# Hybrid decoder layer: memory's 1/rms moved behind its projections, and half of the gMLP value norm moved to ScalarE

## The chip, the cores and the metric

The kernel runs on one core of a Trainium2 chip. A core has five engines with a queue each: TensorE (PE; its weight loads are shown apart as PEld), VectorE (DVE), ScalarE (ACT), GpSimd (POOL) and SyncE (SP, which issues the DMAs here). Each works through its own queue in order and waits for others by semaphores. The metric is the device time of one execution in microseconds.

## What is computed

One layer of a decoder trunk for 1024 tokens of width 1024, in float32, with three sub-layers: a mixer (an S5 state-space group beside a gMLP spatial gate), cross-attention into 256 memory tokens, and a gated FFN with a causal convolution. The change touches two normalisations: that of the gMLP values, per head of 64, and that of the memory.

```python
def rmsnorm(x, g):
    xf = x.astype(jnp.float32)
    xf = xf * lax.rsqrt(jnp.mean(xf * xf, axis=-1, keepdims=True) + RMS_EPS)
    return xf.astype(x.dtype) * g

def chunked_spatial_gate(u, v, g_v, w_s, b_s):
    vh = v.reshape(bsz, nc, CHUNK, GMLP_HEADS, GMLP_HEAD_DIM)
    vh = rmsnorm(vh, g_v.reshape(GMLP_HEADS, GMLP_HEAD_DIM))
    mixed = jnp.einsum('hts,bnshd->bnthd', w_s * mask, vh) + b_s.T[None, None, :, :, None]
    return u * mixed.reshape(bsz, L, D_GMLP)

def memory_cross_attention(h, mem_n, w_q, w_k, w_v, w_o):
    k = (mem_n @ w_k).reshape(bsz, -1, XATTN_HEADS, XATTN_HEAD_DIM)
    v = (mem_n @ w_v).reshape(bsz, -1, XATTN_HEADS, XATTN_HEAD_DIM)
    ...

h = rmsnorm(x, g_mix_pre[l])
s_in, s_gate, g_u, g_vv = jnp.split(h @ w_in[l], splits, axis=-1)
...
mem_n = rmsnorm(mem, g_mem[l])
xa = memory_cross_attention(h, mem_n, w_q[l], w_k[l], w_v[l], w_o[l])
```

## The kernel before

**Products.** Activations lie transposed, channels on partitions and tokens along the row, in tiles of 128x512 (two halves of 512 tokens). Every float32 operand is split into a high part, rounded to the matmul's input type, and a low part that holds the rest; a product is three matmuls (high by high, high by low, low by high), made by `mm3` (L234). ACT makes the high part of a weight tile (the cast of L132), DVE or POOL subtracts it for the low part (L135); for activations the same pair is L253 and L254. Weight tiles come by DMA into four buffers `raw`, and their split parts lie in 13 buffers `w`, so a split waits until PE has done with an older tile.

**The stretch around the change.** In the mixer PE works through, in this order: projections of the S5 input and gate, the gMLP values (`vt`, eight tiles of 128 tokens by 512 channels, with the sums of squares per head in `vss`), gates 0 and 1 of gMLP (`gates`, evicted by the multiply of L1006), the mixing of values along the chunk (`mixing`, L1013, evicted by L1018), gates 2 and 3 (evicted by L1002), then the projections of memory to keys (eight blocks of 128 channels, evicted by ACT copies, L1051) and values (eight tiles, L1059). `v_norm` (L692 to L702) makes 1/rms per head on DVE and multiplies the eight tiles with it, one DVE instruction for a tile (L701), before the mixing.

Memory lies transposed in four tiles of 128x2x256 (two groups of 128 channels, 256 tokens). `mem_norm` makes 1/rms per token, first with tokens on partitions (`r`, one column for each 128 tokens), then spread over all partitions by small matmuls (`mem_bc`, 128x256). `mem_parts` loads a tile, multiplies each half by the gain (a value per partition) and `mem_bc` on DVE (L686), and splits it into high (ACT) and low (POOL).

**S5 beside it.** A side job runs along: eight batches of the state space (`s5_batch`, L540 to L623), each with transposes (L560, copied out by ACT at L564), a product (L575, copied out at L577), halves swapped by DMA, rotations on DVE and POOL (L588 to L597), the scans (L600), a second swap by DMA (L603, L604), the back rotation (L606 on DVE, L607 on POOL, L608 on DVE) and a last product (L618, L619), which reads what L608 wrote. The batches' outputs are read back at L652 and gated at L659.

**The order.** The program's text fixes which side job advances at which tick; then a scheduler in the compiler lays the instructions into the queues by its own estimate of their times. A small edit can thus move other instructions. From the end of the memory projections on the work of PE is the attention, the FFN and the down-projection; its order there is the same in both kernels.

Of the kernel before, what the change touches and what calls it, by code (L numbers as in the profile page):

```python
# [18 lines left out]
AF = mybir.ActivationFunctionType  # L19
ALU = mybir.AluOpType  # L20
AX = mybir.AxisListType

P = 128
# [129 lines left out]
class Builder:  # L153
# [517 lines left out]
    def mem_norm(self):  # L671

        r = yield from self.token_rms("mem", 2, "x")
        yield
        yield
        self.mem_bc = self.bcast(r, 2, "ac")[1]

    def mem_parts(self):
        nc, v, g = self.nc, self.nc.vector, self.nc.gpsimd
        bc = self.mem_bc  # L680
        self.memp = []
        for i in range(4):
            m = self.mem_load(i)
            for j in range(2):
                kt = 2 * i + j
                v.scalar_tensor_tensor(m[:, j], m[:, j], self.gain["g_mem"][:, kt:kt + 1], bc[:, :256],  # L686
                                       ALU.mult, ALU.mult)
            hl = self.pair("m", [P, 2, 256])
            self.split(*hl, m, g)
            self.memp.append(hl)  # L690
            yield

    def v_norm(self, vt, vss):

        nc, v, g = self.nc, self.nc.vector, self.nc.gpsimd
        v.tensor_scalar(vss, vss, 1.0 / 64, EPS, ALU.mult, ALU.add)
        r = self.rsqrt(vss, [P, 64])
        yield
        for i in range(8):
            v3 = vt[i].rearrange("p (h d) -> p h d", d=64)  # L700
            v.tensor_tensor(v3, v3, r[:, 8 * i:8 * i + 8].unsqueeze(2).to_broadcast([P, 8, 64]), ALU.mult)  # L701
            yield  # L702


# [192 lines left out]
    def mixers(self):  # L897
        nc, a, w, ids, xg = self.nc, self.a, self.w, self.ids, self.xg
        v, g = nc.vector, nc.gpsimd
# [4 lines left out]
        for kt in range(KT):  # L904
# [9 lines left out]
            for h in range(2):  # L914
                rh, rl = xg[h][kt]
                for b in range(2):
# [3 lines left out]
                    c = slice(256 * (kt % 2) + P * b, 256 * (kt % 2) + P * b + P)  # L920
# [13 lines left out]
        r = self.value(stat)  # L934
        rstd = [r[:, 4 * h:4 * h + 4] for h in range(2)]
        bc = [self.bcast(rstd[h], 4)[1] for h in range(2)]
# [12 lines left out]
        for b in range(2):  # L949
            part = self.blocks(ids["s"][b])  # L950
            for h in range(2):
                ps = self.bank("sx" if b == 0 else "acc")
# [6 lines left out]
        for b in range(4):  # L959
            part = self.blocks(ids["sg"][b])  # L960
            for h in range(2):
                ps = self.bank()
# [8 lines left out]
        for q in range(2):  # L971
            part = self.blocks(ids["gv"][q], 256)
            for i in range(8):
                ps = self.bank()[:, :256]
                h, c = i // 4, slice((i % 4) * P, (i % 4) * P + P)
# [69 lines left out]
        for b in range(8):  # L1045
            part = self.blocks(ids["k"][b])
            ps = self.bank()[:, :256]
            self.mm3(ps, [(*part(k), *memv(k)) for k in range(8)], ticks=1)
            if b % 2 == 0:
                self.kraw.append(self.slot("m", shape=[P, 2, 256]))  # L1050
            nc.scalar.copy(self.kraw[-1][:, b % 2], ps)  # L1051
        for c in range(4):
            part = self.blocks(ids["v"][c], 256)
            for mt in range(2):
                ps = self.bank()[:, :256]
                self.mm3(ps, [(*memv(k, slice(P * mt, P * mt + P)), *part(k)) for k in range(8)], ticks=1)
                if c % 2 == 0:
                    self.vraw[mt, c // 2] = self.slot("m")
                nc.scalar.copy(self.vraw[mt, c // 2][:, 256 * (c % 2):256 * (c % 2) + 256], ps)  # L1059
        self.memp = None  # L1060
        self.drain(s5)

# [593 lines left out]
```

## Time and the profile before

| | |
|---|---|
| runs | 1346.27, 1342.07, 1339.8 us, median 1342.07 |
| the profiled execution | 1340.39 us, its span 1338.7 us |
| PE, PEld | 1270.3 us (95%), 1076.9 us (80%) |
| DVE | 1062.5 us (79%) |
| ACT | 628.3 us (47%) |
| POOL | 691.0 us (52%) |
| mean granted PE clock | 0.977 |
| DMA | 233.56 MB, mean 174 GB/s |

The profile records one execution. Its span runs from the first to the last instruction; times in rows are counted from its start. A row of the timeline gives start, length, engine, line, operation, out<-in and count, and in brackets the idle time before it and what ended it. Instructions of one engine overlap a little, so the distance between two starts can be shorter than the length of one. A busy PE is not a PE at its peak, since the granted clock is part of it.

### The profile page before, as it was taken

How to read it: one execution, taken by the hardware profiler on the slowest of the kernel's cores; microseconds unless marked ns; L12 is line 12 of the kernel's file. 1: busy time of each engine (PE TensorE's matmuls, PEld its weight loads, DVE VectorE, ACT ScalarE, POOL GpSimd, SP SyncE). 2: the span in 40 equal slices, each digit the busy share in tenths (PEclk: the TensorE clock that was granted, in tenths of full speed). 3: DMA queues.
4: the chain of work that ended last, by engine and by line, in shares of the span. 5: the costliest groups of instructions: out<-in, count | busy, mean ns of one | idle time of the engine just before them, and what ended most of it. 6: DMA issues, size and time to landing. Idle time of an engine off the chain costs nothing. (4 is left out here: it accounts for less than half of the span.)

```text
span 1338.7 us, 19253 instructions
## 1 busy us (share of the span) xinstructions
PE 1270.3 (95%) x6356; PEld 1076.9 (80%) x6356; DVE 1062.5 (79%) x1627; ACT 628.3 (47%) x1176; POOL 691.0 (52%) x523
## 2 busy tenths in 40 slices
PE   9989998779999999889999999999999999999995
PEld 7778987678888788678888878888888888788885
DVE  7968989987558766996657988889998878995477
ACT  7233421245455444454545645555555555546341
POOL 1685445747644734630443838755565315763135
PEclk9989999879999999899999999999999999999997
DMA  9474435348826973451358566645555359666234
GB/s 319 139 206 113 114 95 166 86 125 306 288 94 200 319 244 89 125 187 56 91 163 296 162 222 233 186 144 161 154 167 164 103 162 379 190 201 210 72 92 157
DMA packets 150661, 233.56 MB, mean 174 GB/s; under 512 B 33697, under 2 KB 43041, under 8 KB 150561
## 3 DMA queue, kind: packets, MB, share of 16 engines
q1 hardware_dynamic: 150560, 232.34, 54.5%
q8 instruction: 49, 0.80, 0.3%
q14 instruction: 52, 0.42, 0.1%
HBM read 174.23 MB, written 53.85 MB: 170 GB/s over the span
## 5 line engine op out<-in xcount | busy, mean ns | idle before, releaser
L234 PE MATMUL acc<-b,w 128*128 128x512 f32 x2484 | 597.5, 393 | 10.0 <-DVE sq L965 3.4
L234 PEld LDWEIGHTS acc<-b,w 128*128 128x128 f32 x2484 | 466.6, 190 | 109.1 <-DVE sq L965 3.8
L135 DVE TENSOR_TENSOR w<-raw,w 128x512 fp32r<-128x512 f32 x206 | 203.9, 1000 | 92.6 <-PE acc L234 43.1
L234 PE MATMUL sx<-b,w 128*128 128x512 f32 x873 | 210.1, 390 | 0.7 <-ACT T L1303 0.6
L132 ACT CAST w<-raw 128x512 fp32r<-128x512 f32 x228 | 140.9, 621 | 132.7 <-PE acc L234 70.7
L234 PEld LDWEIGHTS sx<-b,w 128*128 128x128 f32 x873 | 163.6, 188 | 35.5 <-ACT T L1303 1.0
L234 PE MATMUL acc<-T,w 128*128 128x512 f32 x528 | 127.0, 389 | 0.0
L713 POOL TENSOR_TENSOR ac<-ac,sq 128x512 f32<-128x512 f32 x45 | 69.1, 1537 | 103.9 <-ACT sq L712 58.0
L234 PEld LDWEIGHTS acc<-T,w 128*128 128x128 f32 x528 | 99.1, 188 | 20.6
L254 DVE TENSOR_TENSOR w<-b,w 128x512 fp32r<-128x512 f32 x64 | 65.2, 1027 | 30.1 <-PE st L234 15.5
L731 POOL TENSOR_TENSOR m<-m,t 128x512 f32<-128x512 f32 x24 | 40.0, 1698 | 63.7 <-DVE m L730 50.7
L234 PE MATMUL sx<-T,w 128*128 128x512 f32 x264 | 66.5, 389 | 0.0
L234 PEld LDWEIGHTS sx<-T,w 128*128 128x128 f32 x264 | 49.6, 188 | 10.3
L712 ACT ACTIVATE sq<-m 128x512 f32<-128x512 f32 x66 | 41.0, 630 | 34.7 <-DVE ac L713 14.4
L116 POOL TENSOR_TENSOR st<-st,b 128x512 f32<-128x512 f32 x20 | 26.8, 1339 | 56.0 <-DMA st<-in_w_up 35.6
L1242 POOL TENSOR_TENSOR b<-b,m 128x512 f32<-128x512 f32 x22 | 32.2, 1466 | 44.9 <-ACT m L1241 44.7
L253 ACT CAST w<-b 128x512 fp32r<-128x512 f32 x64 | 39.6, 620 | 29.5 <-PE acc L234 18.1
L135 POOL TENSOR_TENSOR w<-raw,w 128x512 fp32r<-128x512 f32 x22 | 30.2, 1377 | 42.5 <-ACT w L132 24.7
L234 PE MATMUL acc<-w,b 128*128 128x256 f32 x384 | 49.3, 285 | 0.0
L1380 POOL TENSOR_TENSOR m<-m,m 128x512 f32<-128x512 f32 x28 | 39.3, 1410 | 18.9 <-DMA m<-in_w_dk 8.4
L730 DVE SCALAR_TENSOR_TENSOR m<-m,gains,st 128x512 f32<-128x512 f32 x32 | 44.5, 1457 | 3.3 <-ACT st L311 3.2
L234 PEld LDWEIGHTS acc<-w,b 128*128 128x128 f32 x384 | 47.0, 191 | 0.1
(360 smaller groups left out, 2335.5 us busy)
## 6 DMA issues: line engine op xcount, KB each, us to landing
raw<-in_w_up SPq DMA_DIRECT2D x68, 256.0 KB, 2.9
cd<-fd SPq DMA_DIRECT2D x44, 256.0 KB, 2.9
b<-sd SPq DMA_DIRECT2D x44, 256.0 KB, 3.9
b<-in_w_up SPq DMA_DIRECT2D x40, 256.0 KB, 2.8
raw<-in_w_out SPq DMA_DIRECT2D x32, 256.0 KB, 2.9
raw<-in_w_q SPq DMA_DIRECT2D x32, 256.0 KB, 2.8
raw<-in_w_o SPq DMA_DIRECT2D x32, 256.0 KB, 2.8
m<-in_w_dk SPq DMA_DIRECT2D x28, 256.0 KB, 4.7
```

What stands on the lines that cost most here:

```text
L116: g.tensor_tensor(p["S4"], p["12"], p["S2"], ALU.subtract)
L132: nc.scalar.copy(hi[:, :w], t[:, :w])
L135: e.tensor_tensor(lo[:, :w], t[:, :w], hi[:, :w], ALU.subtract)
L234: self.pin(nc.tensor.matmul(ps, lhsT=x, rhs=y, start=first and i + j == 0, stop=last and i == n - 1 and j == 2, skip_group_check=go_on))
L253: self.nc.scalar.copy(hi, src)
L254: (e or self.nc.vector).tensor_tensor(lo, src, hi, ALU.subtract)
L712: nc.scalar.activation(sq, src, AF.Square)
L713: (e or nc.gpsimd).tensor_tensor(acc, acc, sq, ALU.add)
L730: v.scalar_tensor_tensor(x, x, self.gain[gpost][:, i:i + 1], bc, ALU.mult, ALU.mult)
L731: g.tensor_tensor(x, x, rs, ALU.add)
L1242: nc.gpsimd.tensor_tensor(val, val, gate, ALU.mult)
L1380: g.tensor_tensor(t[to], t[x], t[y], op)
```

## The change

The values of gMLP: tiles 0, 2, 4, 6 are multiplied by DVE as before, tiles 1, 3, 5, 7 by ACT, head by head, each head with its own scale (eight ACTIVATEs of 128x64 per tile). The memory: the tiles get only the gain, on ACT, and 1/rms is applied where keys and values leave PSUM. For keys tokens lie along the row, so the eight ACT copies become DVE multiplies with `mem_bc`; for values tokens lie on partitions, so the ACT copies become ACTIVATEs with `mem_r` as scale.

```diff
         yield
         yield
+        self.mem_r = r
         self.mem_bc = self.bcast(r, 2, "ac")[1]
 
     def mem_parts(self):
         nc, v, g = self.nc, self.nc.vector, self.nc.gpsimd
-        bc = self.mem_bc
...
                 kt = 2 * i + j
-                v.scalar_tensor_tensor(m[:, j], m[:, j], self.gain["g_mem"][:, kt:kt + 1], bc[:, :256],
-                                       ALU.mult, ALU.mult)
+                nc.scalar.activation(m[:, j], m[:, j], AF.Identity, scale=self.gain["g_mem"][:, kt:kt + 1])
...
             v3 = vt[i].rearrange("p (h d) -> p h d", d=64)
-            v.tensor_tensor(v3, v3, r[:, 8 * i:8 * i + 8].unsqueeze(2).to_broadcast([P, 8, 64]), ALU.mult)
+            if i % 2:
+                for hd in range(8):
+                    nc.scalar.activation(v3[:, hd], v3[:, hd], AF.Identity, scale=r[:, 8 * i + hd:8 * i + hd + 1])
+            else:
+                v.tensor_tensor(v3, v3, r[:, 8 * i:8 * i + 8].unsqueeze(2).to_broadcast([P, 8, 64]), ALU.mult)
...
-            nc.scalar.copy(self.kraw[-1][:, b % 2], ps)
+            v.tensor_tensor(self.kraw[-1][:, b % 2], ps, self.mem_bc[:, :256], ALU.mult)
...
-                nc.scalar.copy(self.vraw[mt, c // 2][:, 256 * (c % 2):256 * (c % 2) + 256], ps)
+                nc.scalar.activation(self.vraw[mt, c // 2][:, 256 * (c % 2):256 * (c % 2) + 256], ps, AF.Identity,
+                                     scale=self.mem_r[:, mt:mt + 1])
```

From here on the file's lines are shifted: L701 of before is L704 (DVE) and L702 (ACT), L1002, L1006, L1013 and L1018 are L1005, L1009, L1016 and L1021, the eviction of keys L1051 is L1054, that of values L1059 is L1062. Lines up to L675 keep their numbers.

**Where the order moves.** First ACT's queue at the norm of v, before:

```order
L132 CAST w_2543<-raw_2298 128x512
L132 CAST w_2594<-raw_2333 128x512
L621 ACTIVATE x_1681<-sx 128x512
L564 COPY x_1713<-sx 128x512
L132 CAST w_2613<-raw_2368 128x512
L577 COPY x_1735<-sx 128x512
```

and after (m_1970 to m_1976 are tiles 1, 3, 5 and 7 of the values, `rs_y` their 1/rms; w_2601 is the weight tile that was w_2594, and w_2627 the one that was w_2613):

```order
L132 CAST w_2543<-raw_2298 128x512
L702 ACTIVATE m_1970<-m_1970,rs_y_2519 128x64 x8
L702 ACTIVATE m_1972<-m_1972,rs_y_2519 128x64 x8
L132 CAST w_2601<-raw_2333 128x512
L702 ACTIVATE m_1974<-m_1974,rs_y_2519 128x64 x8
L702 ACTIVATE m_1976<-m_1976,rs_y_2519 128x64 x8
L621 ACTIVATE x_1681<-sx 128x512
L564 COPY x_1713<-sx 128x512
L132 CAST w_2627<-raw_2368 128x512
L132 CAST w_2785<-raw_2516 128x512
L577 COPY x_1735<-sx 128x512
```

The thirty-two new instructions stand on both sides of one weight cast and ahead of L621 and L564, the copies out of PSUM of two S5 batches. On PE the reader of that copy, L575, moves back past the last seven matmuls of gate 1 and the first two of the mixing.

Next DVE's queue around the third L608 of this stretch (x_1780 is the S5 batch that it finishes), before:

```order
L600 SCALAR_TENSOR_TENSOR x_1780<-r_712,x_1735 128x128 x4
L659 TENSOR_TENSOR k_3135<-k_3125,k_3135 128x4x64
L135 TENSOR_TENSOR w_2758<-raw_2516,w_2757 128x512
L659 TENSOR_TENSOR k_3143<-k_3125,k_3143 128x4x64
L686 SCALAR_TENSOR_TENSOR sq_2813<-sq_2813,gains,ac_1042 128x256 x2
L606 TENSOR_TENSOR x_1780<-x_1780,x_1774 128x512
L135 TENSOR_TENSOR w_2784<-raw_2547,w_2783 128x512
L608 TENSOR_TENSOR x_1780<-x_1780,x_1737 128x512
```

and after:

```order
L600 SCALAR_TENSOR_TENSOR x_1780<-r_712,x_1735 128x128 x4
L1005 TENSOR_TENSOR sq_2825<-acc,st_753 128x512
L135 TENSOR_TENSOR w_2786<-raw_2516,w_2785 128x512
L606 TENSOR_TENSOR x_1780<-x_1780,x_1774 128x512
L608 TENSOR_TENSOR x_1780<-x_1780,x_1737 128x512
L135 TENSOR_TENSOR w_2812<-raw_2547,w_2811 128x512
L1005 TENSOR_TENSOR sq_2869<-acc,st_760 128x512
L659 TENSOR_TENSOR k_3163<-k_3153,k_3163 128x4x64
L659 TENSOR_TENSOR k_3171<-k_3153,k_3171 128x4x64
```

Besides the L686 that are gone, two L659 and one weight split have moved behind L608, and an eviction of a gate (L1002, now L1005) from ahead of the scans to behind them. The reader of L608 on PE, L619, moves ahead by eight matmuls of the gates.

Last, DVE's queue ahead of the fourth L608 (x_1860), before:

```order
L606 TENSOR_TENSOR x_1860<-x_1860,x_1854 128x512
L135 TENSOR_TENSOR w_3235<-raw_3082,w_3234 128x512
L254 TENSOR_TENSOR b_3031<-k_3026,b_3030 128x512
L254 TENSOR_TENSOR b_3049<-k_3044,b_3048 128x512
L608 TENSOR_TENSOR x_1860<-x_1860,x_1839 128x512
```

and after:

```order
L606 TENSOR_TENSOR x_1860<-x_1860,x_1854 128x512
L1054 TENSOR_TENSOR m_3120<-acc,ac_1042 128x256
L254 TENSOR_TENSOR b_3117<-k_3112,b_3116 128x512
L254 TENSOR_TENSOR b_3168<-k_3163,b_3167 128x512
L135 TENSOR_TENSOR w_3309<-raw_3209,w_3308 128x512
L254 TENSOR_TENSOR b_3176<-k_3171,b_3175 128x512
L1054 TENSOR_TENSOR m_3229<-acc,ac_1042 128x256
L608 TENSOR_TENSOR x_1860<-x_1860,x_1839 128x512
```

Five of the eight new evictions, three more weight splits than before and three more L254 now stand ahead of this L608 and behind the third. On PE its reader, L619, moves back by 44 matmuls of the key projection.

## The prediction, made blind

> **What bounds the kernel now.** TensorE (PE) is busy 95% of the span, so the first view is the list of waits, for PE, over the whole span. Columns: who waited for whom, total us, times, longest.
>
> ```profile
> PE sx L619 <- DVE x L608: 17.1, 5, 9.9
> PE acc L234 <- DVE w L135: 7.2, 7, 2.6
> PE acc L1013 <- DVE m L1006: 3.3, 1, 3.3
> ```
>
> All three name VectorE (DVE). Next the stretches, for where: us, then busy time and instructions of PE, PEld, DVE, ACT, POOL, granted PE clock, DMA share, GB/s.
>
> ```profile
> 250.00:275.00 25.00, 18.23 (x111) 16.99 (x111) 22.59 (x18) 9.16 (x17) 23.14 (x15) 0.81 0.25 74
> ...
> 300.00:350.00 50.00, 47.07 (x306) 42.57 (x305) 33.15 (x27) 24.39 (x48) 39.66 (x27) 1.00 0.91 317
> ```
>
> At 250 to 275 us PE idles 6.8 of 25 us, its clock is at 0.81, and DVE and POOL are nearly full; behind 300 us PE is the bound again. The timeline of PE gives the gaps (start, us, in brackets the idle time before, and who ended it):
>
> ```profile
> 206.47 1.05 PE L575 MATMUL sx<-x,x 128*128 128x128 f32 x8
> ...
> 215.63 1.97 PE L1013 MATMUL acc<-k,m 128*64 128x128 f32 x14 [3.26 <-DVE m L1006]
> ...
> 232.98 11.82 PE L234 MATMUL acc<-b,w 128*128 128x512 f32 x51
> 254.69 0.80 PE L619 MATMUL sx<-x,x 128*128 128x127 f32 x2 [9.89 <-DVE x L608]
> ...
> 290.79 0.80 PE L619 MATMUL sx<-x,x 128*128 128x127 f32 x2 [3.83 <-DVE x L608]
> ...
> 293.86 8.97 PE L234 MATMUL acc<-m,w 128*128 128x256 f32 x61
> ...
> 302.66 13.84 PE L234 MATMUL acc<-w,m 128*128 128x256 f32 x114
> ```
>
> These three gaps are 17.0 us (a fourth, for L135, is among the 7.2 above), between the gMLP gates and the end of the key projection at 302.66. Each also lowers the clock afterwards, as a short stretch behind the 9.89 us gap shows:
>
> ```profile
> 256.00:258.00 2.00, 2.00 (x11) 2.00 (x11) 2.00 (x3) 0.52 (x1) 2.00 (x2) 0.50 0.04 10
> ```
>
> So DVE's queue from 198 to 291 us sets the time here, and each of its microseconds ahead of an L608 counts. Behind 302.66 the PE order is unchanged and PE itself is nearly full, so what is won there I carry to the end.
>
> **The norm of v.** Eight DVE multiplies become four on DVE and thirty-two on ScalarE (ACT).
>
> ```profile
> 197.99 5.82 DVE L701 TENSOR_TENSOR m<-m,rs_y 128x512 f32<-128x512 f32 x8
> ...
> 213.03 1.36 DVE L600 TENSOR_TENSOR_SCAN x<-r,x 128x128 f32<-128x128 f32 x4
> ...
> 283.46 1.86 DVE L135 TENSOR_TENSOR w<-raw,w 128x512 fp32r<-128x512 f32 x3
> ```
>
> ACT's, and two of its groups (busy, mean ns of one, idle before):
>
> ```profile
> 200.78 0.58 ACT L564 COPY x<-sx 128x512 f32<-128x512 f32 x1
> ...
> 205.54 0.62 ACT L132 CAST w<-raw 128x512 fp32r<-128x512 f32 x1 [4.17 <-PE acc L234]
> ...
> 1225.83 2.51 ACT L1487 ACTIVATE m<-m,gains 128x256 f32<-128x256 f32 x6
> ```
>
> ```profile
> L1097 ACT COPY m<-acc 128x512 f32<-128x512 f32 x30 | 17.4, 582 | 34.4 <-PE acc L234 34.4
> ...
> L1051 ACT COPY m<-acc 128x256 f32<-128x256 f32 x8 | 2.9, 367 | 3.4 <-PE acc L234 3.4
> ```
>
> DVE loses four instructions of about 0.6 us (three L135 in a row take 1.86): 2.4 us. No 128x64 ACTIVATE with a scale is in the trace. Six of 128x256 take 2.51 us, 0.40 apart ((2.51 - 0.50) / 5, one lasting 0.50); an element costs 0.84 ns ((582 - 367) / 256), so 192 fewer make 0.24 us each. Its bounds are 0.10 (the 0.40 scaled by elements alone) and 0.40 (no cheaper than the wide one). I take 0.24.
>
> The order matters more than the sum. ACT's queue is now sixteen ACTIVATEs, the cast of weights that waited for PE until 205.54, sixteen more, L621, L564. The cast still cannot start before 205.54, so the second sixteen run from 206.16 to 210.0, and L564, done at 201.36 before, ends near 211.2 (two instructions of 0.58 more). L575 needs it. PE ran L575 at 206.47 and now comes to it seven gate matmuls later, at 206.47 + 7 x 0.232 = 208.1 (51 matmuls in 11.82 us), and **waits 3.0 us**. The 3.26 us for L1006 goes in exchange: that multiply, behind a split whose cast follows L564, ends at 211.2 + 0.62 + 0.62 + 0.68 = 213.1, before PE gets there at about 215. The scans now behind it end at 214.5, where they ended at 214.39, so the second L608 stays where it was. **Term: 0**, from a gain of 2.4 (ACT holds up nothing) to a loss of 2.6 (16 x 0.16 at the upper price).
>
> The Trainium skill (ScalarE: Activation LUTs, section Rules for kernel authors) budgets about 0.3 us per ACTIVATE and 0.83 ns per element, and advises VectorE for a plain multiply. By that the estimate is 0.35 each, L564 1.8 us later and the whole gain near 3 instead of 5; the slope agrees with the rows' 0.84 ns, the fixed part not with the 0.40 us between the wide ones.
>
> **The memory tiles.** Eight L686 leave DVE and become eight ACTIVATEs with the gain as scale. On ACT they cost 3.2 us (0.40 each); it was busy 9.16 us of the 25 in the stretch above, which hides them. Were that cover gone, the first key block would be late (rival c). On DVE:
>
> ```profile
> L686 DVE SCALAR_TENSOR_TENSOR sq<-sq,gains,ac x8: 471/1314/1702, 228.1 to 256.0; 128x256 f32<-128x256 f32 x8
> L1002 DVE TENSOR_TENSOR sq<-acc,st x4: 676/678/692, 244.0 to 270.9; 128x512 f32<-128x512 f32 x4
> ```
>
> The first columns are the shortest, median and longest in ns. DVE's timeline:
>
> ```profile
> 228.06 3.32 DVE L686 SCALAR_TENSOR_TENSOR sq<-sq,gains,ac 128x256 f32<-128x256 f32 x2
> ...
> 237.75 1.54 DVE L686 SCALAR_TENSOR_TENSOR sq<-sq,gains,ac 128x256 f32<-128x256 f32 x2
> ...
> 244.58 3.01 DVE L600 TENSOR_TENSOR_SCAN x<-r,x 128x128 f32<-128x128 f32 x4
> 247.52 0.59 DVE L659 TENSOR_TENSOR k<-k,k 128x256 f32<-128x256 f32 x1
> 248.02 0.68 DVE L135 TENSOR_TENSOR w<-raw,w 128x512 fp32r<-128x512 f32 x1
> 248.62 0.61 DVE L659 TENSOR_TENSOR k<-k,k 128x256 f32<-128x256 f32 x1
> 249.15 0.87 DVE L686 SCALAR_TENSOR_TENSOR sq<-sq,gains,ac 128x256 f32<-128x256 f32 x2
> 250.59 0.69 DVE L606 TENSOR_TENSOR x<-x,x 128x512 f32<-128x512 f32 x1 [0.57 <-DMA x<-x]
> 251.20 1.76 DVE L135 TENSOR_TENSOR w<-raw,w 128x512 fp32r<-128x512 f32 x1
> 252.89 1.74 DVE L608 TENSOR_TENSOR x<-x,x 128x512 f32<-128x512 f32 x1
> 254.56 2.89 DVE L686 SCALAR_TENSOR_TENSOR sq<-sq,gains,ac 128x256 f32<-128x256 f32 x2
> ...
> 290.05 0.68 DVE L608 TENSOR_TENSOR x<-x,x 128x512 f32<-128x512 f32 x1
> ```
>
> and one row of POOL's:
>
> ```profile
> 250.63 1.78 POOL L607 TENSOR_TENSOR x<-x,x 128x512 f32<-128x512 f32 x1 [3.62 <-DMA x<-x]
> ```
>
> Between the second and third L608, ahead of the scans, leave two pairs, 3.32 + 1.54; one L1018 (0.7, like L1002) now stands earlier, one L1002 (0.7) later. The scans end at 247.59 - 6.3 = 241.3. From there the path is no longer DVE's own: the swap by DMA (250.59 - 247.59 = 3.0), POOL's L607 (1.78), L608 (1.74). The third pair, the two L659 and the L135 that were there are out of the way. In SP's queue the two DMAs of the swap now stand ahead of the last reads of S5 output, in POOL's L607 ahead of a split; with DMA at 0.25 of its share in that stretch I count both at nothing, and up to 1.5 either way through the later order of the values' weights, which now stand ahead of the down-projection's. The third L608 ends at 247.8, where it was 254.63. PE has eight fewer matmuls ahead of it, comes at 244.8 - 1.9 = 242.9 and waits about 5 us instead of 9.89, still long enough for the lower clock.
>
> That price is the traced one. L686 took 0.47 us at best and 1.70 while POOL worked, and L1002, which reads PSUM, 0.68 throughout. If POOL's work merely slows the next instruction instead, a pair is worth 0.87, not 2.43 on the mean, and the third L608 ends 3.1 later, at 250.9. The Trainium skill (SBUF — State Buffer, section SBUF: two separate sides) says just this: DVE with two SBUF inputs and a GpSimd instruction exclude each other for a whole instruction. By that rule the sum goes by the lower price, below; the two rows agree.
>
> **Keys and values.** Eight L1051 copies leave ACT for DVE as multiplies from PSUM (new L1054); the values only get a scale on the same ACT instruction, at most 0.1 us each on an engine with idle time. A 128x256 multiply from PSUM is not in the trace: below 0.68 (L1002, twice the size), above 0.24, which this one of 64 columns takes:
>
> ```profile
> 197.57 0.24 DVE L566 TENSOR_TENSOR s5ka<-sx,k 128x64 f32<-128x64 f32 x1
> ```
>
> By columns that is 0.43 in between, 0.40 as spacing. From the third to the fourth L608 DVE took 290.73 - 254.63 = 36.1. Out: the last L686 pair, 2.89. In: two L659 1.20, the L135 of 1.76, two more L135 and three L254 at 0.62 (3.1), five L1054 (2.0). Makes 41.3; the fourth L608 ends at 289.1 instead of 290.73. But 44 matmuls of the key projection now stand ahead of it in PE's queue, 17 behind instead of 61. Behind it then come 3.07 (290.79 to 293.86) and 17 x 0.147 = 2.5: the key projection ends at 294.7, **8.0 earlier**. By the lower price (third L608 at 250.9, 0.87 instead of 2.89) the fourth ends at 294.2 and the projection at 299.8, **2.9 earlier**.
>
> I take the middle, 5: POOL's amount of work stays, which speaks for the lower end; but POOL idled 3.62 ahead of L607, so with casts that come sooner it also ends sooner. Total: 0 - 5 = **-5 us**: 1340.39 of the profiled execution (its span of 1338.7 and 1.7 around it) becomes 1335.4; the median of the runs shown lies 1.7 above it, so **1337**.
>
> **Rivals.** (a) Larger: the traced price holds, and waits become so short that the clock stays up. 8.0, and up to 3 of half-clock work saved behind the last L608: 9 to 11, near 1331. For it: half-speed stretches behind each gap; against: the new waits of 3 and 5 us are no shorter than those that lowered it. (b) Eaten up: lower price, and the ACT queue at 0.40, or weights of the values that come late because DMA is at 0.91 there: 2.9 - 2.6 = 0.3, near 1341. (c) Slower: L1054 turns DVE's queue into a convoy. It waits for PE to finish a key block, and behind it stand the L135 that PE needs next. It stands about four weight tiles ahead of PE and costs nothing as long as PE lags less; it decides once PE is later than that, say by a memory tile that waits in ACT's queue. Then five waits of a block (24 x 0.105 = 2.5; 192 matmuls of this form in all) are 12.5, less the 5: 7.5 slower, near 1349. Against it: ACT idles much of the stretch.
>
> **Numbers.** A measurement of this kernel tells about 0.5%, 6.7 us, from no change. Forecast (a gain of 2 to 6.7) 0.37; (a) 0.33; (b) 0.17; (c) 0.13. So faster 0.33, same 0.54, slower 0.13. Best bounds: 8.0 + 2.4 + 3 = 13 faster, 1329; at the other end (b) entire and half the way into (c), 1346.
>
> **What would show it.** PE's waits: one for ACT L564 at L575 of about 3 us in place of L1006's; the third L608 at 248 to 251 with a wait near 5; the end of the key projection at 295 to 300, and the same distance from there to the end. Wrong if DVE sits idle for PE at L1054, if the 128x64 ACTIVATEs are over 0.4 us apart, or if PE waits for the values' weights.

## The result, and the profile after

Measured beside each other on one chip, five runs each: before 1342.07 us (1338.65 to 1346.27), after 1331.63 us (1328.18 to 1335.54), ratio 0.990, 95% interval 0.9872 to 0.9928. Two later measurements of the changed kernel gave 0.9928 (0.9903 to 0.9953) and 0.991 (0.9889 to 0.993). The change is faster by about 1%, 10 to 13 us, twice what was forecast. The profiled execution took 1332.37 us, its span 1330.7, its mean granted clock 0.981.

PE's waits of the changed kernel over the whole span (total us, times, longest):

```profile
PE sx L619 <- DVE x L608: 11.4, 6, 5.8
PE acc L234 <- DVE w L135: 7.9, 7, 3.3
```

The 17.1 us for L608 are 11.4, the wait for L1006 has left the head of the list, and the waits for weight splits are no shorter (7.2 before). The stretch of which the prediction quoted 6.8 us of idle PE (us, then busy time of PE, PEld, DVE, ACT, POOL, clock, DMA share, GB/s):

```profile
250.00:275.00 25.00, 19.66 (x124) 17.84 (x122) 19.72 (x16) 6.26 (x11) 23.70 (x15) 0.91 0.21 62
```

The clock rose from 0.81 to 0.91, and DVE is no longer full (22.59 before); POOL is, as it was (23.14 before). PE's timeline shows the same gaps, and the end of the key projection in its last row:

```profile
209.72 1.16 PE L575 MATMUL sx<-x,x 128*128 128x128 f32 x8
...
215.06 0.65 PE L1016 MATMUL acc<-k,m 128*64 128x128 f32 x6 [0.29 <-DVE sq L1021]
...
221.48 0.49 PE L619 MATMUL sx<-x,x 128*128 128x127 f32 x2 [2.03 <-DVE x L608]
...
247.95 0.80 PE L619 MATMUL sx<-x,x 128*128 128x127 f32 x2 [5.80 <-DVE x L608]
...
270.94 2.17 PE L234 MATMUL acc<-m,w 128*128 128x256 f32 x12 [3.35 <-DVE w L135]
...
290.40 0.49 PE L619 MATMUL sx<-x,x 128*128 128x127 f32 x2 [0.67 <-DVE x L608]
...
294.81 5.44 PE L234 MATMUL acc<-w,m 128*128 128x256 f32 x44
```

For comparing runs, take the end of the norm's 1/rms (the last L271 of 128x64 ahead of the multiplies; 197.95 before, 199.13 after) as zero. The key projection ends 104.71 us behind it before and 95.68 after: 9.0 us less. In windows of 1 us over this stage, PE idle is 21.1 us before and 15.9 after, and the half clock (PE's busy time times one minus the clock, summed) costs 9.8 and 4.3. From the end of the projections of keys and values to the end of the span it is 1010.7 and 1010.1 us: what was won was carried to the end.

DVE's timeline of the changed kernel at the third L608 and behind it:

```profile
246.16 1.74 DVE L608 TENSOR_TENSOR x<-x,x 128x512 f32<-128x512 f32 x1 [1.15 <-POOL x L607]
...
255.92 1.19 DVE L135 TENSOR_TENSOR w<-raw,w 128x512 fp32r<-128x512 f32 x1
262.39 1.94 DVE L590 TENSOR_TENSOR x<-x,x 128x512 f32<-128x512 f32 x1 [5.28 <-POOL x L589]
...
289.67 0.67 DVE L608 TENSOR_TENSOR x<-x,x 128x512 f32<-128x512 f32 x1
```

The third L608 ends 7.9 us earlier than before, the fourth 1.6. In between DVE now stands 5.28 us for POOL, which works off splits of the mixer and memory ahead of L588 and L589:

```profile
256.51 2.98 POOL L254 TENSOR_TENSOR b<-m,b 128x512 fp32r<-128x512 f32 x2
259.46 1.47 POOL L588 TENSOR_TENSOR x<-k,k 128x512 f32<-128x512 f32 x1
260.89 1.46 POOL L589 TENSOR_TENSOR x<-k,k 128x512 f32<-128x512 f32 x1
```

So a new wait took the place of an old one, and yet the time fell. Which part did it?

### The profile page after: what moved, and what is told of

It reads as the page before. It is cut to its first block, busy times and chain, and to the rows that moved or that the text cites. A ratio compares the mean times of both kernels' runs of the same rounds, so it can differ in the third digit from the quotient of the medians.

```text
span 1330.7 us, 19282 instructions
## 1 busy us (share of the span) xinstructions
PE 1266.7 (95%) x6356; PEld 1073.7 (81%) x6356; DVE 1049.5 (79%) x1623; ACT 638.6 (48%) x1208; POOL 693.2 (52%) x523
## 4 chain that ended last, share of the span: by engine, by line
PE 49%; DVE 4%; DMA 1%; issue 1%; ACT 1%; POOL 0%; SPq 0%; DVEq 0%; POOLq 0%; ACTq 0%
PE acc L234 29%; PE sx L234 17%; PE st L234 2%; DVE w L135 1%; DVE m L733 1%; DVE m L788 0%; PE st L281 0%; DMA rs<-x1d 0%; DVE m L790 0%; DMA p1d<-t 0%; PE st L308 0%; DVE m L779 0%; DVE ac L1548 0%; DMA raw<-in_w_up 0%; DVE ac L716 0%
## 5 line engine op out<-in xcount | busy, mean ns | idle before, releaser
L135 DVE TENSOR_TENSOR w<-raw,w 128x512 fp32r<-128x512 f32 x206 | 197.5, 967 | 92.9 <-PE acc L234 38.9
L254 DVE TENSOR_TENSOR w<-b,w 128x512 fp32r<-128x512 f32 x64 | 59.7, 944 | 25.2 <-PE st L234 10.3
```

Source lines behind the costliest of these rows:

```text
L135: e.tensor_tensor(lo[:, :w], t[:, :w], hi[:, :w], ALU.subtract)
L254: (e or self.nc.vector).tensor_tensor(lo, src, hi, ALU.subtract)
```

## The experiments

All kernels below were timed in five rounds beside the kernel before; ratios are against it. The positions are us behind the end of the norm's 1/rms, from one profiled execution each; idle and half clock are PE's, up to the end of the key projection.

| run | ratio (95%) | third L608 | fourth L608 | keys end | idle | half clock |
|---|---|---|---|---|---|---|
| before | 1 | 56.7 | 92.8 | 104.7 | 21.1 | 9.8 |
| after | 0.990 (0.9872 to 0.9928) | 48.8 | 91.2 | 95.7 | 15.9 | 4.3 |
| e8, after again | 0.9928 (0.9903 to 0.9953) | 48.7 | 90.8 | 95.3 | 15.6 | 4.3 |
| e16, after again | 0.991 (0.9889 to 0.993) | 48.6 | 90.8 | 96.4 | 14.0 | 7.6 |
| e1, norm alone | 0.996 (0.9945 to 0.9975) | 56.6 | 88.0 | 96.5 | 16.4 | 5.9 |
| e2, memory part alone | 0.9954 (0.9939 to 0.9969) | 54.4 | 95.4 | 98.8 | 15.6 | 8.6 |
| e3, gain back on DVE | 0.9933 (0.9916 to 0.9951) | 56.9 | 91.4 | 98.1 | 17.2 | 6.2 |
| e4, same, one operand | 0.9934 (0.9915 to 0.9953) | 51.3 | 92.8 | 96.2 | 14.7 | 6.0 |
| e5, evictions alone | 0.9975 (0.9959 to 0.999) | 56.6 | 95.0 | 101.1 | 18.3 | 7.8 |
| e6, keys by ACT copy | 0.9947 (0.9928 to 0.9967) | 48.7 | 87.3 | 97.5 | 16.3 | 7.1 |
| e7, all values on ACT | 0.9944 (0.9924 to 0.9964) | 51.7 | 93.3 | 98.0 | 16.6 | 4.5 |
| e13, norm, DVE refilled | 0.9963 (0.9946 to 0.9979) | 59.0 | 90.4 | 98.6 | 17.4 | 6.8 |

The three profiles of the changed kernel say how far such figures repeat: the third and fourth L608 within 0.4 us, the keys' end within 1.2, the split between idle and half clock only within 3.3.

### The parts alone (e1 to e4)

e1 is the kernel before with the new lines of `v_norm` alone, e2 the change without them. e3 puts the multiply of `mem_parts` back on DVE:

```diff
-                nc.scalar.activation(m[:, j], m[:, j], AF.Identity, scale=self.gain["g_mem"][:, kt:kt + 1])
+                v.scalar_tensor_tensor(m[:, j], m[:, j], self.gain["g_mem"][:, kt:kt + 1], self.mem_bc[:, :256],
+                                       ALU.mult, ALU.mult)
```

and e4 puts it there with the gain alone:

```diff
-                nc.scalar.activation(m[:, j], m[:, j], AF.Identity, scale=self.gain["g_mem"][:, kt:kt + 1])
+                v.tensor_scalar(m[:, j], m[:, j], self.gain["g_mem"][:, kt:kt + 1], None, ALU.mult)
```

> Only the value norm is changed (odd tiles on ScalarE); memory as before. In the profile of the change the cast between the two groups of sixteen ACTIVATEs did not wait (203.00, right behind the first group), L564 ended at 208.4 and PE came to L575 at 209.7 without a wait; the 3.26 us wait for L1006 is gone too, but the second L608 moved only 1.4 us (from 23.7 to 22.3 us behind the end of the norm's rsqrt). Theory A (L686 was worth what it took in the trace, 8.6 us): the norm gives little, 1 to 2 us less than before. Theory B (L686 was worth 0.44 us each, 3.5 in all, the rest handed on by POOL to the next instruction): then most of the 10 us must come from the norm and the moved order, 4 to 6 us less than before here.

> Only the memory part is changed (gain on ScalarE, 1/rms at the evictions of keys and values); all eight value tiles stay on DVE. Theory A: 7 to 9 us less than before. Theory B: 3 to 5 us less than before. By both the 3.26 us wait of PE for L1006 comes back; by A it costs nothing at the end of the key projection, since DVE's queue sets that.

> The changed kernel with the eight multiplies by gain and 1/rms back on DVE in the old form, evictions as in the change, so that the memory's 1/rms is applied twice. This prices L686 alone. Theory A: 7 to 9 us more than the change, close to before. Theory B: 3 to 4 us more than the change.

> The changed kernel with the gain multiplied on DVE by a tensor_scalar, which reads one operand from SBUF and a value per partition. Theory A with contention as its cause: such an instruction is not slowed by POOL, about 0.35 us each, 2 to 3 us more than the change, and its rows show no spread. Theory B: the same 2 to 3 us, so that this run differs from the run with the two-operand form by 5 to 6 us under A and by 1 us under B.

The norm alone brings 0.4% (5.4 us of 1344): inside theory B's 4 to 6, above theory A's 1 to 2. The memory part alone brings 6.2, between A's 7 to 9 and B's 3 to 5. They add up to the whole, within their intervals. Taking L686 off DVE is worth little within the change: e3 lies 0.05 to 0.33% above the three measurements of it, 1 to 4 us (with intervals of about 2.5 us either way), though its third L608 comes 8 us later:

```profile
254.76 1.75 DVE L608 TENSOR_TENSOR x<-x,x 128x512 f32<-128x512 f32 x1
290.31 0.68 DVE L608 TENSOR_TENSOR x<-x,x 128x512 f32<-128x512 f32 x1
```

The next one is level with the change again (91.4 and 91.2). Theory A, a full 8.6 us for L686, falls: what DVE gains at the third L608 it spends waiting for POOL behind it (0.77 us at L590 in e3, 5.28 in the change). The kernel with the one-operand form (e4) is as fast as that with the two-operand one, where theory A had 5 to 6 us between them. The rows of e4 spread as well, from 0.32 to 1.59 us (0.45 to 1.71 in e3), so the spread does not hang on the second operand.

### The evictions (e5, e6)

e5 is the kernel before with the new lines at L1051 and L1059 alone. e6 undoes one of them in the change:

```diff
-            v.tensor_tensor(self.kraw[-1][:, b % 2], ps, self.mem_bc[:, :256], ALU.mult)
+            nc.scalar.copy(self.kraw[-1][:, b % 2], ps)
```

> The kernel before with only the evictions of the change: keys by DVE multiplies with memory's 1/rms, values with it as ACT's scale. The eight L686 stay on DVE in their old form, so 1/rms enters twice and the output is not the reference's. DVE loses nothing here and gains eight instructions of 0.41 us. Theory C (the evictions pay by themselves: the fourth product of S5 on PE, L619, stands 31 matmuls of the key projection later, so its wait of 3.8 us and the half clock behind it go): 3 to 5 us below the kernel before, no wait of PE at the fourth L608, the third L608 unchanged at 56.7 us behind the norm's end. Theory D (each part pays only through DVE's load): 0 to 3 us slower than before, since DVE does more.

> The changed kernel with the keys evicted by ACT copies as before; memory's 1/rms is left out of the keys, so the output is not the reference's. All order up to the key projection is that of the change; PE's last L619 stands 32 matmuls of the key projection earlier again. Theory C: 3 to 5 us slower than the change, that is 5 to 8 us below the kernel before, with a wait of 3 to 5 us at the fourth L608. Theory D: DVE has 3.3 us less to do, so as fast as the change or up to 2 us faster, 10 to 13 below the kernel before.

Theory C holds in sign both times: 3.4 us alone, and 2.6 us between e6 and e8 on the same chip; each of these two has an interval of about 2.5 us or more either way, so this difference is not clear of noise. In e6 the order is that of the change up to the key projection; then PE waits where the change has 0.67:

```profile
286.08 0.80 PE L619 MATMUL sx<-x,x 128*128 128x127 f32 x2 [2.98 <-DVE x L608]
```

In e5 a wait of 2.75 stayed, which theory C had excluded. DVE has more to do by eight instructions of 0.41 us, and yet the kernel is faster. Up to the end of the key projection PE's order differs from that of before in one thing, that the last product of S5 stands 31 matmuls later (in e6, 32 earlier than in the change); DVE and ACT have some splits and casts in another order. So this gain looks like one of order; that ACT, freed of eight copies, has a share in it is not excluded.

### The norm: DVE's time or the order (e13, e7)

e13 is e1 with the time given back. On every engine its order is that of e1, but for four added instructions:

```diff
+                v.tensor_tensor(v3, v3, v3, ALU.max)
```

> The kernel before with only the norm of v of the change (odd tiles on ACT), and four DVE instructions added that change nothing (the maximum of an even tile with itself, 128x512, 0.6 us each or more): DVE has the load of before again, 2.4 us or more, while the order on all engines is that of the norm alone, which was 0.996 of before. Theory P (the gain is DVE's freed time): most of the 5 us are gone, ratio 0.998 to 1.001, the third L608 some 2 us later than with the norm alone (56.6 us behind the norm's end). Theory O (the gain is the order that the scheduler makes of it: a pair of L686 and an eviction pulled ahead of the third L608, six gate matmuls ahead of PE's wait there): ratio 0.995 to 0.998, third L608 within 1 us.

```profile
201.06 1.60 DVE L706 TENSOR_TENSOR m<-m 128x512 f32<-128x512 f32 x1
203.78 1.88 DVE L706 TENSOR_TENSOR m<-m 128x512 f32<-128x512 f32 x3
```

The four took 3.5 us, about what DVE had been freed of (eight L701 took 5.82 us, four take 2.50), and the third L608 came 2.4 later than in e1. Yet the ratio is 0.9963 against 0.996 (0.4 us, with an interval of some 3 us either way), and of the 8.2 us that e1 wins up to the keys' end 6.1 are left. Theory O holds but for the third L608, where only P had 2 us: the norm pays mostly by the order that the scheduler makes of it. That order: behind the third L608 no pair of L686 is left (all eight stand ahead), and one eviction fewer, so that DVE goes from the third to the fourth L608 in 31.4 us in e1 and e13, 36.1 before; on PE six more gate matmuls stand ahead of the third wait, and 42 key matmuls instead of 61 behind the fourth. Which of these moves pays was not tested one by one.

e7 changes one line of the change, `if i % 2:` into `if True:`.

> The changed kernel with all eight tiles of the values normalised by ACT, head by head: 64 ACTIVATEs of 128x64. At 0.24 us each ACT has 15.7 us of them ahead of the mixing, where the change has 7.9, and DVE 2.4 less. My prediction's first term said that ACT's queue holds up the copies out of PSUM (L564, L577) and so PE: by that theory 4 to 8 us slower than the change, with PE waiting 3 us or more for ACT or for the values. Rival (what DVE loses is what counts, and ACT's idle time covers the rest): 1 to 3 us faster than the change.

It is 2 us slower than e8 on the same chip, within both intervals: neither theory is shown. The scheduler set the copies between the ACTIVATEs, and neither L575 nor the mixing waited for ACT, so the blocked queue that I feared did not come about even with 64:

```profile
206.31 2.26 ACT L702 ACTIVATE m<-m,rs_y 128x64 f32<-128x64 f32 x9
208.48 0.58 ACT L621 ACTIVATE x<-sx 128x512 f32<-128x512 f32 x1
208.95 0.57 ACT L564 COPY x<-sx 128x512 f32<-128x512 f32 x1
209.42 3.94 ACT L702 ACTIVATE m<-m,rs_y 128x64 f32<-128x64 f32 x16
```

### The clock behind a gap (e9, e10, e14)

The kernel before, with matmuls that nothing needs ahead of the third L619, 24, 80 and 56 of them, in one and the same order:

```diff
-        py = self.bank("sx")
+        py = self.bank("sx"); [nc.tensor.matmul(py[:, :P], lhsT=z[:, i % 4], rhs=s[:, i % 4], start=True, stop=True) for i in range(56 if b == 6 else 0)]
```

> The kernel before with 24 extra matmuls of 128x128 on PE (their output is overwritten) ahead of L618 and L619 of the third S5 batch. They also change the scheduler's order: 32 of the gate matmuls move behind this L619, so PE comes to it some 7 us earlier and, with 24 x 0.13 = 3.2 us of filling, waits about 12 us for the third L608, at the half clock afterwards. It is there for comparison with the run of 80: against the kernel before, any sign by every theory.

> As the run with 24 extra matmuls, and in the same order on every engine, but with 80 of them: PE does 56 x 0.13 = 7.4 us more work that nothing needs, all of it while it would wait for the third L608. Theory (it is PE's idleness that lowers the granted clock behind a gap, so the half clock that the change saved came with the shorter waits): the matmuls behind the gap run at full clock, half-clock loss of the stage 2 to 4 us less than with 24, and the kernel 2 to 4 us faster than with 24. Rival (the clock follows something else, or the gap's length alone counts): as fast as with 24, or slower by up to 2 us.

> As the runs with 24 and 80 extra matmuls and in the order of the one with 24, but with 56 of them: at 0.226 us each 12.7 us, which end as the third L608 ends, so they cost PE nothing. Theory (idleness lowers the clock, and that costs time): the clock stays at 1.00 behind this gap, and the key projection ends 1.5 to 2.5 us earlier than with 24. Rival (the time comes back at the fourth L608, whose wait was 6.25 us with 24): that wait grows by the same 2 us, and the time is that of 24 within 1 us.

Ratios 1.0017 (1.0003 to 1.0031), 1.0059 (1.0041 to 1.0077) and 1.0079 (1.0058 to 1.0101). My price of the filling was wrong. The rows count two records for each of these matmuls (80 stand as x160), which I had read as two matmuls: they take 0.226 us each, so 24 leave a wait of 7.34 us, not the 12 expected, 80 outlast it by 5 us, and 56 fit. The filling with 80, and PE's rows with 24, then with 56, from the third L619 to the gate matmuls and the fourth L619:

```profile
241.36 18.10 PE L615 MATMUL sx<-x,x 128*128 128x128 f32 x160 [1.84 <-DVE x L553]
```

```profile
254.60 0.79 PE L619 MATMUL sx<-x,x 128*128 128x127 f32 x2 [7.34 <-DVE x L608]
...
257.66 8.70 PE L234 MATMUL acc<-b,w 128*128 128x512 f32 x32
266.46 5.04 PE L234 MATMUL acc<-b,w 128*128 128x512 f32 x21
...
282.06 0.80 PE L619 MATMUL sx<-x,x 128*128 128x127 f32 x2 [6.25 <-DVE x L608]
```

```profile
255.25 0.49 PE L619 MATMUL sx<-x,x 128*128 128x127 f32 x2 [0.22 <-DVE x L608]
...
257.55 7.56 PE L234 MATMUL acc<-b,w 128*128 128x512 f32 x32
265.20 5.04 PE L234 MATMUL acc<-b,w 128*128 128x512 f32 x21
...
282.39 0.80 PE L619 MATMUL sx<-x,x 128*128 128x127 f32 x2 [7.84 <-DVE x L608]
```

and the windows there, 24 first (the clock is the third number from the end):

```profile
254.00:258.00 4.00, 3.40 (x15) 3.40 (x16) 2.93 (x5) 0.62 (x1) 1.93 (x1) 0.50 0.29 66
```

```profile
254.00:258.00 4.00, 3.78 (x24) 3.55 (x23) 3.60 (x5) 0.73 (x2) 1.93 (x2) 1.00 0.29 66
```

From the start of the third L619 to the start of the row with 21 matmuls, the same matmuls take 11.9 us behind an idle gap of 7.34 us and 9.95 behind one of 0.22. So idleness lowers the clock, at a price of 1.9 us for this gap. The Trainium skill (TensorE: Matmul & The Clock Gate, section What's actually happening) has the clock at half after an idle window of some 3.4 us and full again after a busy one of that length; the run agrees with the half (0.50), while the length of 3.4 us was not measured here.

What becomes of these 1.9 us is nearer to the rival. The fourth wait grew from 6.25 to 7.84 us. The key projection ended 105.0 instead of 106.4 us behind the norm, just short of the theory's 1.5 us and hardly more than such figures scatter, and the projections of keys and values together ended at 136.2 instead of 136.4. The run with 80 says it more plainly: PE does 12.7 us more work in it than with 24, and the two projections end at 136.4 all the same. Time saved on PE is kept only where PE is the bound next. Behind these projections the rival fails too: by the ratios e14 is some 8 us slower than e9, and e10 some 6. The profiled execution of e14, the longest of its six, took 13 us longer there than that of e9, with longer waits in the attention, although DVE, ACT and POOL have the same order. Why is open.

### Can the new wait be taken away? (e11, e12, e15; e8 and e16 beside them)

e11 moves four splits of the mixer from POOL to DVE, e12 and e15 (the same kernel twice) those of memory. In their order:

```diff
-                self.split(*hl, gu.pop((b, h)), g)
+                self.split(*hl, gu.pop((b, h)), g if h else v)
```

```diff
-            self.split(*hl, m, g)
+            self.split(*hl, m)
```

> The changed kernel with the low parts of the mixer's first half (four L254 of 128x512, tokens 0 to 511) made by DVE instead of POOL. In the changed kernel DVE idles 5.28 us at L590 for POOL's L588 and L589, ahead of which stand three of these L254. Theory (POOL's queue is the new bound behind the third L608): L589 ends 4 to 5 us earlier, the wait at L590 goes below 2 us, the fourth L608 comes 2 to 4 us earlier, and the kernel is 2 to 4 us faster than the change. Rival (DVE and POOL are both full there, so that work moved to DVE comes back as DVE time): the four L254 take 1.5 us each on DVE, the fourth L608 no earlier, time as the change within 1.5 us or slower.

> The changed kernel with memory's low parts (four L254 of 128x2x256) made by DVE instead of POOL. DVE gets four instructions of 0.7 to 1.75 us, two or three of them ahead of the third L608, POOL loses four of 1.3 to 1.75. Theory (POOL's queue is the new bound behind the third L608): the third L608 1 to 3 us later than in the change, the wait at L590 below 2 us, the fourth L608 1 to 3 us earlier, the kernel 1 to 3 us faster than the change. Rival (DVE's queue still sets the third L608 and what follows from it): 1 to 4 us slower than the change.

> The changed kernel with memory's low parts on DVE once more, beside the change on the same chip. If the 0.9917 against 0.9928 was more than chance: 1 to 3 us faster than the change. If not: within 1 us of it.

> The changed kernel once more, beside the others on the same chip: 9 to 13 us below the kernel before. What its profile gives for the stage (95.7 us from the end of the norm's 1/rms to the end of the key projection, PE idle 15.9, half clock 4.3) shows how far such figures repeat: within 1 us by every theory.

> The changed kernel beside it: 9 to 11 us below the kernel before by every theory, as in the two measurements so far.

e11: 0.9952 (0.9935 to 0.997). e12: 0.9917 (0.9898 to 0.9937), e15: 0.9912 (0.9894 to 0.993). The wait at L590 goes in e11 and shrinks to 2.81 us in e12:

```profile
261.49 1.95 DVE L590 TENSOR_TENSOR x<-x,x 128x512 f32<-128x512 f32 x1 [2.81 <-POOL x L589]
```

and the fourth L608 comes 5 to 6 us earlier in both (85.5 and 85.6). Still neither beats the change: e15 is level with e16 on the same chip, e11 is 3 to 7 us slower. (The profiled execution of e11 was its shortest, so it does not show where these were lost.) PE's last L619 now stands 49 (e11) and 30 (e12) matmuls earlier and waits 2.0 and 4.2 us again. The wait for POOL at L590 was real, but taking it away only moved the waiting; no version beat the change.

## Why the prediction was right or wrong

**What bounds it: half right.** DVE's queue does decide PE's gaps, but "each of its microseconds ahead of an L608 counts" was false: 8 us at the third L608 are worth about 2 at the keys' end (e3: 98.1 against 95.3 to 96.4), and a fourth L608 5 to 6 us earlier brought nothing in e12, where PE's product stood earlier too. DVE and POOL meet again behind each L608.

**The norm of v: the step that failed.** The term put at 0 was worth 5.4 us alone, about half of the whole gain. First, its wait at L575 came of a row put to the wrong cast. The row at 205.54 is the cast that stands behind L564, whose tile became w_2627, not the one between the ACTIVATEs; in the kernel before that one ran here:

```profile
193.53 0.62 ACT L132 CAST w<-raw 128x512 fp32r<-128x512 f32 x1 [3.46 <-PE acc L234]
```

In the change it waits for nothing:

```profile
199.16 3.93 ACT L702 ACTIVATE m<-m,rs_y 128x64 f32<-128x64 f32 x16 [7.90 <-DVE rs_y L271]
203.00 0.61 ACT L132 CAST w<-raw 128x512 fp32r<-128x512 f32 x1
203.51 3.94 ACT L702 ACTIVATE m<-m,rs_y 128x64 f32<-128x64 f32 x16
207.35 0.58 ACT L621 ACTIVATE x<-sx 128x512 f32<-128x512 f32 x1
207.82 0.58 ACT L564 COPY x<-sx 128x512 f32<-128x512 f32 x1
```

L575 did not wait, and the 3.26 us for L1006 went without an exchange. The price was right: 16 in 3.93 us with the last 0.34 long are 0.24 apart. Second, I followed the term to the second L608 and closed the sum there (1.4 us earlier, not 0). The gain lies behind the third, in what the scheduler pulled ahead: from the third to the fourth L608 DVE takes 31.4 us instead of 36.1, with DVE's time given back too (e13).

**The memory tiles: the direction right, the account wrong.** Third L608: forecast 247.8 by the traced price, 250.9 by the lower one; it came at 197.95 + 48.8 = 246.7 on the scale of before. That looks like the traced price, but neither part does it alone (56.6 with the norm, 54.4 with memory's part), and within the change L686 is worth 1 to 4 us (e3) of the 8.6 that its eight rows take. PE's wait there, 5.80, was forecast as about 5, and the clock did fall behind it:

```profile
248.00:251.00 3.00, 3.00 (x14) 3.00 (x15) 3.00 (x4) 1.95 (x4) 2.10 (x2) 0.50 0.51 171
```

**Keys and values: right in size, partly by luck.** L1054 took 0.41 us (0.43 forecast), with the next instruction 0.33 behind its start (0.40 forecast); the fourth L608 ended at 289.2 on that scale (289.1 forecast by the traced price), the keys at 293.6 (294.7). But this sum was made for memory's part with nothing from the norm, and memory's part alone (e2) has the third L608 at 252.4, the fourth at 293.4 and the end of the keys at 296.7. The full change reached the forecast marks with the norm's help. The memory part alone, evictions included, gave 6.2 us (interval 4.2 to 8.2), inside the 2.9 to 8.0 of the forecast. So the middle of 5 was not the mistake; the zero beside it was.

**The clock: counted only in a rival.** Half-clock loss is 2 to 6 us less in the three profiles of the change. e14 shows that such a loss is real, and also that what is saved of it can go again at the next wait, so no fixed part of the gain is put to it here.

**Rivals.** (a), larger, is what came, in size; of its two reasons the shorter waits hold, the traced price as a gain of its own does not (e3). (b) would have had ACT at 0.40 a piece: it was 0.24. (c), the convoy at L1054, did not occur: DVE never stood idle for PE there. Its price was also too low: a matmul of 128x256 takes 0.12 us in the rows (114 in 13.84 us), not 0.105, so a block is 2.9 us and not 2.5.

## What to carry to other kernels

Where a scheduler lays the queues, price a freed microsecond by what is pulled into its place, up to the next point where the engines meet and beyond: nearly half of this gain was the order that came with the norm, and it stayed when the time was given back. Before a wait in the trace is handed to a moved instruction, match that row by its place among its neighbours, not by its line. An earlier milestone (an L608, a shorter wait, a clock that stays up) was a gain here only where PE was the bound behind it.

## What was not expected of the hardware

An ACTIVATE of 128x64 with a scale per partition lasts 0.34 us, but follows another at 0.24 us. The Trainium skill (ScalarE: Activation LUTs, section What ACT_TABLE_LOAD costs) gives both: 280 ns with a per-partition operand, 0.833 ns an element, an overlap of about 93 ns back to back, an estimate of 0.33 and 0.24; the budget rule that the prediction quoted leaves the overlap out.
